# First block's startup: weights and modulation weights loaded each by its own free buffers, x transposed unscaled, contraction cut 3+5+8

## The chip, the cores and the metric

The kernel runs on one core of a Trainium2 chip. The metric is the device time of one execution in microseconds. Names of engines are those of the profile: PE (matrix), DVE (vector), ACT (scalar), POOL, and SP, which here only issues DMA.

## What is computed

The reference runs two transformer blocks, one after the other, on a sequence of 256 tokens of width 2048, in fp32. The change touches the beginning of the first block alone:

```python
mod = jax.nn.silu(c) @ w_ada[l] + b_ada[l]
shift1, scale1, gate1, shift2, scale2, gate2 = jnp.split(mod, N_MOD, axis=-1)

h = rms_norm(x, norm1_w[l]) * (1.0 + scale1[:, None]) + shift1[:, None]
proj = h @ w_in[l]
u_pool, q, k, v, g_a, g_b = jnp.split(proj, split_at, axis=-1)
```

`w_ada` has 2048 x 12288 elements and `w_in` 2048 x 8192. Behind that come a pooling branch, an attention branch, gates, an output projection and a feed-forward part; the second block has the same frame with other branches.

## The kernel before

All weights stream through one fixed sequence of blocks of 1 MiB, each a 128x4x512 fp32 tile `raw`. A matrix product is made of three products of rounded halves: ACT casts half a block (128x1024) to `hi` (fp32r, L201), DVE subtracts it from `raw` to get `lo` (L209), and PE runs hi, lo and hi again for each 128 of the contraction, each of 4 units of a block and each half of the tokens: 24 matmuls of 512 columns a block (L303 to L305). Half a block is called a sub. hi and lo have four buffers each, `raw` four.

Nothing is scheduled by the framework here: each engine executes in the order in which the code is written. `run` walks the subs; ahead of sub s it prepares hi and lo up to sub s+3 (`prep_to`, with `LOOK` = 3), then it issues the matmuls of sub s and, where a product ends there, its eviction.

The modulation is not a matrix product on PE. c is passed through silu and spread over all 128 partitions as `cb` (four matmuls with one active row, L497, copied from PSUM on DVE, L548). One column of 128 entries of `mod` is then one DVE operation, `ada_product` (L177): a 128x2048 tile of `w_ada` (1 MiB, `ada`, two buffers) times `cb`, summed along the row. In what follows that is a product.

The contraction of 2048 is cut in 16 slices k. Slice k of h, h tile k, needs products k and 16 + k; `h_tile` (L561) makes two columns `sAB` from them (DVE, L563, L565), and `modulate` (L381) makes act's high part on ACT (L384), hm on DVE (L385) and act's low part on DVE (L386).

So as not to need all 32 products at once, the first 48 blocks of `w_in` run in three chunks of the contraction (`CHUNKS` = 0, 4, 10, 16). In each chunk twelve column groups of 512 (ga 0 to 3, q, k, u and v, two each) are run over the chunk's k; in the first two chunks the four ga go k by k, in the last all go group by group. ga 0 and ga 1 keep their PSUM (`held`, tag ms); the others have two pairs of PSUM buffers in turn (tag acc) and put the partial sum in SBUF at each chunk's end: chunk 0 copies it on ACT (L607), the later ones add it on DVE (L609). Blocks 0 to 11 are chunk 0, 12 to 29 chunk 1, 30 to 47 chunk 2.

One queue holds the order of the weight blocks, the products and the calls; `when` says ahead of which block a product stands: two ahead of each of blocks 0 to 3, then from block 5 one each 1.1 blocks, from 19.5 one each 1.05. `pump` issues loads on SP strictly in that queue's order, and stops at the first one whose buffer isn't free. `prep_hi` executes the products and calls that stand ahead of a block before it casts the block's first half; so product, h tile, hi and lo stand in this order on DVE and ACT.

Of the kernel before, what the change touches and what calls it, by code (L numbers as in the profile page):

```python
# [18 lines left out]
P = 128  # L19
# [12 lines left out]
ADAB = 2  # L32

# [12 lines left out]
class Seg:  # L46
# [5 lines left out]
    def __init__(self, lhs, ks, end=None, tag="acc", end_tt=None, tail=2):  # L52
        self.lhs, self.ks, self.end, self.tag, self.end_tt = lhs, list(ks), end, tag, end_tt
        self.tail = tail if end_tt else 0
        self.acc = None
        self.left = [len(self.ks)] * 2

# [6 lines left out]
class Net:  # L64
    def __init__(self, ctx, tc, A):
# [21 lines left out]
        self.q_dma = 0  # L87
# [69 lines left out]
    def pump(self):  # L157

        while self.q_dma < len(self.queue):
            kind, what, src = self.queue[self.q_dma]  # L160
            if kind == "w":
                if what - self.prepped // 2 >= RAWB:
                    return
                t = self.rawp.tile([P, 4, 512], F32, tag="raw", name="raw")
                self.nc.sync.dma_start(out=t, in_=src)
                self.raw[what] = t
            elif kind == "a":
                if len(self.ada_dma) - self.ada_done >= ADAB:
                    return
                t = self.adap.tile([P, D], F32, tag="ada", name="ada")  # L170
                self.nc.sync.dma_start(out=t, in_=src)
                self.ada_dma.append(t)
            self.q_dma += 1
# [120 lines left out]
    def unit(self, seg, k, hi, lo, tts=(0, 1)):  # L294
        if seg.acc is None:
            seg.acc = [self.psp.tile([P, 512], F32, tag=seg.tag, name="acc") for _ in range(2)]
        for tt in tts:
            first = seg.left[tt] == len(seg.ks)
# [4 lines left out]
            self.nc.tensor.matmul(a, xh, hi, start=first, stop=False)  # L303
            self.nc.tensor.matmul(a, xh, lo, start=False, stop=False)  # L304
            self.nc.tensor.matmul(a, xl, hi, start=False, stop=last)  # L305
            if last and seg.end_tt:
                while self.pre_end:
                    self.pre_end.pop()()
                seg.end_tt(a, tt)
        if seg.end and not any(seg.left):  # L310
            seg.end(seg.acc)

# [171 lines left out]
    def setup(self):  # L484
        nc, fix, A = self.nc, self.fix, self.A

        row = self.mixp.tile([1, 2 * D], F32, tag="B", name="crow")
# [19 lines left out]
        self.mask = self.t2([P, P], name="mask")  # L507
        nc.sync.dma_start(out=self.mask, in_=A["mask"])
# [7 lines left out]
        self.mod2 = fix.tile([P, 96], F32, tag="mod2", name="mod2")  # L516

# [10 lines left out]
    def block1(self):  # L528
# [12 lines left out]
        junk = mp.tile([P, D], F32, tag="u", name="junk")  # L541
        for tt in range(2):
            nc.scalar.activation(junk, x[:, tt, :], AF.Square, accum_out=tot[:, tt:tt + 1])
            r = self.rstd(tot[:, tt:tt + 1], 1, D)
            nc.vector.tensor_scalar(out=x[:, tt, :], in0=x[:, tt, :], scalar1=r, scalar2=None, op0=ALU.mult)
            if tt == 0:
                for i, ps in enumerate(self.cbps):
                    nc.vector.tensor_copy(self.cb[:, i * 512:(i + 1) * 512], ps)  # L548
        nc.vector.scalar_tensor_tensor(out=wb, in0=self.pk("b_ada", 16, 16), scalar=1.0, in1=self.pk("norm1_w"),
                                       op0=ALU.add, op1=ALU.mult)  # L550
        xT = mp.tile([P, KD, S], F32, tag="B", name="xT")

        for tt in range(2):
            for c in range(4):
# [4 lines left out]
        self.at(6, self.setup2)  # L559

        def h_tile(k):  # L561
            sAB = self.fix.tile([P, 2], F32, tag="sAB", name="sAB", bufs=2)
            nc.vector.tensor_scalar(out=sAB[:, 0:1], in0=mod[:, 16 + k:17 + k], scalar1=self.pk("norm1_w", k, 1),  # L563
                                    scalar2=wb[:, k:k + 1], op0=ALU.mult, op1=ALU.add)
            nc.vector.tensor_tensor(out=sAB[:, 1:2], in0=mod[:, k:k + 1], in1=self.pk("b_ada", k, 1), op=ALU.add)  # L565
            self.modulate(xT[:, k, :], get(k // 4)[:, k % 4, :, :], sAB[:, 0:1], sAB[:, 1:2])
# [58 lines left out]

        held = {("ga", g): Seg(h_lhs, range(16), lambda acc, g=g: gate_a(g, acc), "ms") for g in range(2)}
        w = A["win1"]
        chunk = {}
# [3 lines left out]
        for c, (b0, every) in enumerate(((5, 1.1), (19.5, 1.05)), 1):  # L632
            for i in range(2 * (ch[c + 1] - ch[c])):
                when.setdefault(int(b0 + every * i), []).append((ch[c] + i // 2, i % 2))
        for nb, bl in enumerate(startup_blocks()):
# [7 lines left out]
            for key, k in bl:  # L643
                c = max(i for i in range(len(ch)) if ch[i] <= k)
                if key not in held and (key, c) not in chunk:
                    chunk[key, c] = Seg(h_lhs, range(ch[c], ch[c + 1]), part_end(key, c))
# [794 lines left out]
CHUNKS = (0, 4, 10, 16)  # L1441


def startup_blocks():
# [4 lines left out]
    for c in range(len(ch) - 1):  # L1449
# [4 lines left out]
        else:  # L1454
            rest = [keys[i] for i in (2, 3, 4, 0, 5, 1, 6, 8, 7, 9, 10, 11)]
# [99 lines left out]
```

## Time and profile before

| | us |
|---|---|
| median of 3 runs | 2512.89 |
| lowest and highest | 2510.8, 2512.9 |
| profiled execution | 2512.52 |
| its span, first to last instruction | 2510.7 |
| PE busy in the span | 2478.9 |
| PE idle in the first 300 us | 18.4 |

The page gives shares of the whole span; the windows view cuts the span in stretches and shows each engine's busy time in each, and there the idle time of PE is found at the start. The groups by line say how often an operation ran and how long the engine was idle before it; the timeline says when.

### The profile page before, as it was taken

What the parts mean: (1) busy time and instruction counts of PE and PEld (TensorE: products, weight loads), DVE (VectorE), ACT (ScalarE), POOL (GpSimd) and SP (SyncE); (2) the same over time, 40 slices, a digit from 0 to 9 for tenths busy, and PEclk for the clock granted to TensorE, in tenths of its full rate; (3) what the DMA queues carried; (4) which work ended last, traced back from release to release, by engine and by line L of the source; (5) the groups of instructions that cost most, each with busy time, mean ns of one, the idle gap of its engine ahead of it and who ended that gap; (6) DMA issues with size and microseconds to landing.
All of it is one profiled execution on the core that took longest, in us unless ns stands there. A gap on an engine that the chain in (4) does not pass through costs nothing.

```text
span 2510.7 us, 29213 instructions
## 1 busy us (share of the span) xinstructions
PE 2478.9 (99%) x11332; PEld 2047.1 (82%) x11332; DVE 1807.3 (72%) x2122; ACT 1259.9 (50%) x1727; POOL 4.0 (0%) x8
## 2 busy tenths in 40 slices
PE   7999999999999999999999999999999999999999
PEld 5778888887888888888887888888788888888887
DVE  7898888888875777787778878766676655456554
ACT  4536645445545444534446556665554453453443
POOL 0000000000000000000000000000000000000000
PEclk9999999999999999999999999999999999999999
DMA  9988678977887778787776655666567655555553
GB/s 358 369 322 318 243 297 323 394 306 286 303 317 284 303 315 316 287 333 306 294 276 222 249 214 211 221 232 223 212 252 278 259 200 194 208 185 191 193 190 130
DMA packets 93580, 666.24 MB, mean 265 GB/s; under 512 B 10817, under 2 KB 11521, under 8 KB 12929
## 3 DMA queue, kind: packets, MB, share of 16 engines
q1 hardware_dynamic: 93442, 664.38, 69.7%
q8 instruction: 89, 1.46, 0.2%
q14 instruction: 49, 0.40, 0.0%
HBM read 660.11 MB, written 4.23 MB: 265 GB/s over the span
## 4 chain that ended last, share of the span: by engine, by line
PE 88%; DVE 6%; ACT 3%; DMA 1%; issue 1%; SPq 0%; ACTq 0%; DVEq 0%
PE acc L303 28%; PE acc L305 28%; PE acc L304 28%; DVE lo L209 2%; DVE ada L177 2%; PE ms L348 1%; DMA raw<-in_win 1%; ACT hi L201 1%; PE ms L1178 1%; PE ms L855 1%; PE ms L1292 0%; ACT hm L1396 0%; PE ms L1410 0%; DVE res L395 0%; PE ms L762 0%
## 5 line engine op out<-in xcount | busy, mean ns | idle before, releaser
L209 DVE TENSOR_TENSOR lo<-raw,hi 128x1024 fp32r<-128x1024 f32 x848 | 1027.6, 1223 | 594.7 <-ACT hi L201 591.6
L201 ACT CAST hi<-raw 128x1024 fp32r<-128x1024 f32 x848 | 884.7, 1051 | 868.1 <-PE acc L305 825.0
L303 PE MATMUL acc<-hi,act 128*128 128x512 f32 x2208 | 875.5, 396 | 7.6 <-ACT hi L201 6.1
L304 PE MATMUL acc<-lo,act 128*128 128x512 f32 x2208 | 864.3, 391 | 9.8 <-DVE lo L209 9.8
L305 PE MATMUL acc<-hi,act 128*128 128x512 f32 x2208 | 863.1, 391 | 0.0
L304 PEld LDWEIGHTS acc<-lo,act 128*128 128x128 f32 x2208 | 416.3, 189 | 99.7 <-DVE lo L209 17.2
L303 PEld LDWEIGHTS acc<-hi,act 128*128 128x128 f32 x2208 | 416.2, 188 | 94.9 <-ACT hi L201 8.4
L305 PEld LDWEIGHTS acc<-hi,act 128*128 128x128 f32 x2208 | 415.9, 188 | 88.1 <-DVE act L1401 0.7
L177 DVE CUSTOM_DVE_ANT_0 ada<-ada,cb 128x2048 f32<-128x2048 f32 x192 | 438.3, 2284 | 0.5 <-DMA ada<-in_ada 0.5
L303 PE MATMUL acc<-hi,f 128*128 128x512 f32 x1024 | 399.1, 390 | 0.0
L305 PE MATMUL acc<-hi,f 128*128 128x512 f32 x1024 | 398.4, 389 | 0.0
L304 PE MATMUL acc<-lo,f 128*128 128x512 f32 x1024 | 398.4, 389 | 0.0
L305 PEld LDWEIGHTS acc<-hi,f 128*128 128x128 f32 x1024 | 192.2, 188 | 40.1
L304 PEld LDWEIGHTS acc<-lo,f 128*128 128x128 f32 x1024 | 192.2, 188 | 39.9
L303 PEld LDWEIGHTS acc<-hi,f 128*128 128x128 f32 x1024 | 192.2, 188 | 39.1
L384 ACT ACTIVATE act<-xT,sAB 128x256 fp32r<-128x256 f32 x16 | 9.6, 601 | 86.2 <-DVE sAB L565 86.2
L419 ACT ACTIVATE relu<-acc 128x512 f32<-128x512 f32 x64 | 37.7, 590 | 29.0 <-PE acc L305 29.0
L350 DVE TENSOR_TENSOR f<-ms,f 128x512 fp32r<-128x512 f32 x64 | 41.0, 683 | 3.1 <-ACT f L349 3.1
L395 DVE TENSOR_TENSOR res<-acc,gate 128x512 f32<-128x512 f32 x32 | 22.0, 689 | 28.2 <-PE acc L305 28.2
L398 ACT ACTIVATE res<-x 128x512 f32<-128x512 f32 x24 | 15.2, 633 | 52.6 <-DVE x L396 52.6
L420 ACT ACTIVATE relu<-relu 128x512 f32<-128x512 f32 x64 | 40.5, 633 | 2.0
L349 ACT CAST f<-ms 128x512 fp32r<-128x512 f32 x64 | 34.4, 589 | 13.8 <-PE ms L348 13.8
(245 smaller groups left out, 1266.8 us busy)
## 6 DMA issues: line engine op xcount, KB each, us to landing
raw<-in_ff SPq DMA_DIRECT2D x240, 1024.0 KB, 5.6
ada<-in_ada SPq DMA_DIRECT2D x192, 1024.0 KB, 5.8
raw<-in_win SPq DMA_DIRECT2D x120, 1024.0 KB, 6.5
raw<-in_ff1p SPq DMA_DIRECT2D x16, 1024.0 KB, 4.8
raw<-in_wa SPq DMA_DIRECT2D x8, 1024.0 KB, 6.9
raw<-in_wb SPq DMA_DIRECT2D x8, 1024.0 KB, 9.1
raw<-in_wop SPq DMA_DIRECT2D x8, 1024.0 KB, 6.9
raw<-in_wo SPq DMA_DIRECT2D x8, 1024.0 KB, 9.7
```

The costliest lines, as they stand in the source:

```text
L177: self.nc.vector.tensor_tensor_reduce(out=t, in0=t, in1=cb(), scale=1.0, scalar=0.0, op0=ALU.mult, op1=ALU.add, accum_out=mod[:, j:j + 1])
L201: self.nc.scalar.copy(hi, src)
L209: self.nc.vector.tensor_tensor(out=lo, in0=src, in1=hi.bitcast(F32), op=ALU.subtract)
L303: self.nc.tensor.matmul(a, xh, hi, start=first, stop=False)
L304: self.nc.tensor.matmul(a, xh, lo, start=False, stop=False)
L305: self.nc.tensor.matmul(a, xl, hi, start=False, stop=last)
L348: nc.tensor.transpose(ps[:, i, :], src[:, i * P:(i + 1) * P], self.ident)
L349: nc.scalar.copy(dst[:, :, 0, :], ps)
L350: nc.vector.tensor_tensor(out=dst[:, :, 1, :], in0=ps, in1=dst[:, :, 0, :].bitcast(F32), op=ALU.subtract)
L419: nc.scalar.activation(r, acc[tt], AF.Relu)
L420: nc.scalar.activation(r, r, AF.Square)
L855: mm = lambda *a, **kw: nc.tensor.matmul(*a, skip_group_check=True, **kw)
```

## The change

- `pump` keeps a list of weight loads and one of modulation loads. Each is issued when a buffer of its own kind is free, the one that stands first in the queue first. The first four modulation tiles lie in the four buffers of act (`ADAX`), which are empty then, so six modulation loads and four weight loads can be out at the start.
- The mask's load moves from the start to sub 4, and `setup2`, which reads it, from sub 6 to sub 10.
- Two matmuls of a blank 128x512 tile stand ahead of the four that spread c.
- x is no longer scaled by the reciprocal norm before it is transposed. The scale of each token is spread over the partitions by two transposes as `rows`, and h tile multiplies by it: hm is one operation of two tensors and a column on DVE, then act's high part on ACT, then its low part on DVE. The two columns of `sAB` are made on ACT.
- `CHUNKS` is 0, 3, 8, 16: blocks 0 to 8, 9 to 23, 24 to 47. In the last chunk ga 2 and ga 3 go k by k first. `when` starts at block 3 with one product a block, and at block 13 with one each 0.92.
- Chunk 1 no longer adds on DVE: when a pair of PSUM buffers is evicted, ACT copies the next group's partial sum from SBUF into it (`back`, `heir`), the matmuls add onto it, and ACT copies the sum out again. Chunk 2 adds on DVE as before.

```diff
+ADAX = 4
...
+    def open(self, net):
+
+        self.acc = [net.psp.tile([P, 512], F32, tag=self.tag, name="acc") for _ in range(2)]
+        if self.init:
+            self.init(self.acc)
...
+        if self.loads is None:
+            self.loads = {kind: [i for i, e in enumerate(self.queue) if e[0] == kind][::-1] for kind in "wa"}
+        ws, ads = self.loads["w"], self.loads["a"]
+        while True:
+            n = len(self.ada_dma)
+            w = ws and self.queue[ws[-1]][1] - self.prepped // 2 < RAWB
+            a = ads and (n < ADAX + ADAB or n - self.ada_done < ADAB)
+            if w and (not a or ws[-1] < ads[-1]):
+                _, b, src = self.queue[ws.pop()]
+                t = self.raw[b] = self.rawp.tile([P, 4, 512], F32, tag="raw", name="raw")
+            elif a:
+                src = self.queue[ads.pop()][2]
+
+                if n < ADAX:
+                    t = self.actp.tile([P, D], F32, tag="act", name="ada")
+                else:
+                    t = self.adap.tile([P, D], F32, tag="ada", name="ada")
                 self.ada_dma.append(t)
-            self.q_dma += 1
+            else:
+                return
+            self.nc.sync.dma_start(out=t, in_=src)
...
         if seg.end and not any(seg.left):
             seg.end(seg.acc)
+            if seg.heir:
+                seg.heir.open(self)
...
+        ps = self.ms()
+        for i in range(2):
+            nc.tensor.matmul(ps, blank[:, 0:P], blank, start=i == 0, stop=i == 1)
...
-            nc.vector.tensor_scalar(out=x[:, tt, :], in0=x[:, tt, :], scalar1=r, scalar2=None, op0=ALU.mult)
...
+            nc.scalar.activation(sa, mod[:, 16 + k:17 + k], AF.Identity, bias=wb[:, k:k + 1],
+                                 scale=self.pk("norm1_w", k, 1))
+            nc.scalar.activation(sb, mod[:, k:k + 1], AF.Identity, bias=self.pk("b_ada", k, 1))
+            h = self.t2([P, S], name="hm")
+            nc.vector.scalar_tensor_tensor(out=h, in0=src, scalar=sa, in1=rows, op0=ALU.mult, op1=ALU.mult)
+            nc.scalar.activation(dst[:, 0, :], h, AF.Identity, bias=sb)
+            nc.vector.scalar_tensor_tensor(out=dst[:, 1, :], in0=h, scalar=sb, in1=dst[:, 0, :].bitcast(F32),
+                                           op0=ALU.add, op1=ALU.subtract)
...
-                    if c == 0:
+                    if c < len(ch) - 2:
                         nc.scalar.copy(d[:, tt, :], acc[tt])
...
+        def back(key):
+            def init(acc):
+                d = part(key)
+                for tt in range(2):
+                    nc.scalar.copy(acc[tt], d[:, tt, :])
+            return init
...
-        for c, (b0, every) in enumerate(((5, 1.1), (19.5, 1.05)), 1):
+        for c, (b0, every) in enumerate(((3, 1.0), (13, 0.92)), 1):
...
+                    if 0 < c < len(ch) - 2:
+                        seg.init = back(key)
+                        order[-3].heir = seg
...
-CHUNKS = (0, 4, 10, 16)
+CHUNKS = (0, 3, 8, 16)
...
-            rest = [keys[i] for i in (2, 3, 4, 0, 5, 1, 6, 8, 7, 9, 10, 11)]
+            out += [(g, k) for k in ks for g in keys[2:4]]
+            rest = [keys[i] for i in (0, 4, 1, 5, 6, 8, 7, 9, 10, 11)]
```

Where instructions stand now. First SP, the queue of loads at the program's start; `ada` is a modulation load, `raw` a weight load. Before:

```order
L508 DMA mask<-in_mask 128x128
L171 DMA ada<-in_ada 128x2048 x2
L165 DMA raw<-in_win 128x2048
L171 DMA ada<-in_ada 128x2048 x2
L165 DMA raw<-in_win 128x2048
L171 DMA ada<-in_ada 128x2048 x2
L165 DMA raw<-in_win 128x2048
```

After:

```order
L531 DMA pkt<-in_pk 128x293
L189 DMA ada<-in_ada 128x2048 x2
L189 DMA raw<-in_win 128x2048
L189 DMA ada<-in_ada 128x2048 x2
L189 DMA raw<-in_win 128x2048
L189 DMA ada<-in_ada 128x2048 x2
L189 DMA raw<-in_win 128x2048 x4
L189 DMA ada<-in_ada 128x2048 x2
L189 DMA raw<-in_win 128x2048
```

Six modulation loads and six weight loads now stand ahead of the seventh modulation load (the first of the last `ada` row); the mask's load has moved behind.

Second DVE, from the product ahead of block 13's lo on; the `ISA` rows with `ada` are the products (each with the read-out of its column), `hm` and `act` belong to an h tile, `lo` x2 is a block. Before, blocks 13 to 15:

```order
L177 ISA ada,mod_113<-ada,cb 128x2048
L177 ISA mod_113 128x1
L209 TENSOR_TENSOR lo<-raw,hi 128x1024 x2
L177 ISA ada,mod_113<-ada,cb 128x2048
L177 ISA mod_113 128x1
L563 TENSOR_SCALAR sAB<-mod_113,pkt,wb 128x1
L565 TENSOR_TENSOR sAB<-mod_113,pkt 128x1
L385 TENSOR_SCALAR hm<-xT,sAB 128x256
L386 TENSOR_TENSOR act<-hm,act 128x256
L209 TENSOR_TENSOR lo<-raw,hi 128x1024 x4
```

After, blocks 13 to 15:

```order
L193 ISA ada,mod_115<-ada,cb 128x2048
L193 ISA mod_115 128x1
L193 ISA ada,mod_115<-ada,cb 128x2048
L193 ISA mod_115 128x1
L601 SCALAR_TENSOR_TENSOR hm<-xT,sAB,rrow 128x256
L603 SCALAR_TENSOR_TENSOR act<-hm,sAB,act 128x256
L225 TENSOR_TENSOR lo<-raw,hi 128x1024 x2
L193 ISA ada,mod_115<-ada,cb 128x2048
L193 ISA mod_115 128x1
L225 TENSOR_TENSOR lo<-raw,hi 128x1024 x2
L193 ISA ada,mod_115<-ada,cb 128x2048
L193 ISA mod_115 128x1
```

In before blocks 14 and 15 have one product between them; in after block 13 has two, and blocks 14 and 15 one each (block 15's h tile and lo follow these rows).

Third ACT, in after, from block 13 to block 16: `sAB` and `act` are an h tile's, `hi` a sub each, `gap<-acc` the eviction of ga 2 and ga 3 at the end of chunk 1, `acc<-qk` the partial sums put back for q and k:

```order
L217 CAST hi<-raw 128x1024 x4
L597 ACTIVATE sAB<-mod_115,wb,pkt 128x1
L599 ACTIVATE sAB<-mod_115,pkt 128x1
L602 ACTIVATE act<-hm,sAB 128x256
L217 CAST hi<-raw 128x1024
L645 COPY gap<-acc 128x512 x2
L668 COPY acc<-qk 128x512 x2
L645 COPY gap<-acc 128x512 x2
L668 COPY acc<-qk 128x512 x2
L217 CAST hi<-raw 128x1024 x3
```

In before, where the adds of chunk 1 are on DVE, ACT has nothing but h tiles and hi between chunk 0's last eviction and block 31:

```order
L384 ACTIVATE act<-xT,sAB 128x256
L201 CAST hi<-raw 128x1024 x6
L384 ACTIVATE act<-xT,sAB 128x256
L201 CAST hi<-raw 128x1024 x6
L384 ACTIVATE act<-xT,sAB 128x256
L201 CAST hi<-raw 128x1024 x4
```

The evictions of block 13 and the copies back now stand on ACT behind the h tile and the first hi of block 15, and ahead of its second hi.

## Rows read from the trace of the kernel before

**Rows 1.** The page, part 1: busy us, share of the span, instructions.

```profile
PE 2478.9 (99%) x11332; PEld 2047.1 (82%) x11332; DVE 1807.3 (72%) x2122; ACT 1259.9 (50%) x1727; POOL 4.0 (0%) x8
```

**Rows 2.** Busy time by windows: busy us, granted clock, DMA share, GB/s.

```profile
0.00:10.00 10.00, 5.63 (x7) 2.49 (x8) 1.74 (x8) 8.52 (x8) 0.20 (x4) 1.00 0.80 301
...
20.00:30.00 10.00, 8.38 (x24) 6.34 (x25) 8.49 (x12) 3.72 (x6) 0.00 (x0) 0.66 0.92 360
...
200.00:250.00 50.00, 50.00 (x225) 41.27 (x224) 38.33 (x46) 31.31 (x64) 0.00 (x0) 1.00 0.79 298
```

**Rows 3.** Waits of PE in the first 205 us: total, times, longest.

```profile
PE acc L304 <- DVE lo L209: 6.5, 9, 0.8
PE acc L303 <- ACT hi L201: 6.1, 3, 3.1
...
PE acc L303 <- DVE gap L609: 1.1, 1, 1.1
```

**Rows 4.** Groups on DVE, 41.0 to 167.7 us: count, busy, mean ns, idle before.

```profile
L209 DVE TENSOR_TENSOR lo<-raw,hi 128x1024 fp32r<-128x1024 f32 x43 | 51.6, 1222 | 10.8 <-ACT hi L201 10.8
L177 DVE CUSTOM_DVE_ANT_0 ada<-ada,cb 128x2048 f32<-128x2048 f32 x20 | 45.7, 2284 | 0.5 <-DMA ada<-in_ada 0.5
L386 DVE TENSOR_TENSOR act<-hm,act 128x256 fp32r<-128x256 f32 x10 | 4.3, 426 | 2.2 <-ACT act L384 2.2
...
L609 DVE TENSOR_TENSOR qk<-acc,qk 128x512 f32<-128x512 f32 x6 | 3.8, 680 | 0.0
...
L609 DVE TENSOR_TENSOR gap<-acc,gap 128x512 f32<-128x512 f32 x4 | 2.5, 682 | 0.0
```

**Rows 5.** DVE in order of time: start, us, operation, idle before.

```profile
25.61 2.29 DVE L177 CUSTOM_DVE_ANT_0 ada<-ada,cb 128x2048 f32<-128x2048 f32 x1
27.83 0.08 DVE L177 DVE_READ_ACCUMULATOR2_ANT mod<- 128x1 f32 x1
...
29.89 2.36 DVE L209 TENSOR_TENSOR lo<-raw,hi 128x1024 fp32r<-128x1024 f32 x2 [0.51 <-ACT hi L201]
32.17 2.29 DVE L177 CUSTOM_DVE_ANT_0 ada<-ada,cb 128x2048 f32<-128x2048 f32 x1
...
40.94 2.28 DVE L177 CUSTOM_DVE_ANT_0 ada<-ada,cb 128x2048 f32<-128x2048 f32 x1
```

**Rows 6.** ACT in order of time, same columns.

```profile
10.40 0.29 ACT L334 ACTIVATE rstd<-sstot,eps 128x1 f32<-128x1 f32 x1
...
28.32 0.60 ACT L384 ACTIVATE act<-xT,sAB 128x256 fp32r<-128x256 f32 x1 [6.28 <-DVE sAB L565]
28.83 1.98 ACT L201 CAST hi<-raw 128x1024 fp32r<-128x1024 f32 x2
...
54.60 2.04 ACT L607 COPY gap<-acc 128x512 f32<-128x512 f32 x4
56.51 1.08 ACT L201 CAST hi<-raw 128x1024 fp32r<-128x1024 f32 x1
```

**Rows 7.** DVE again: a lo behind ACT's copies.

```profile
57.62 1.23 DVE L209 TENSOR_TENSOR lo<-raw,hi 128x1024 fp32r<-128x1024 f32 x1 [1.10 <-ACT hi L201]
```

**Rows 8.** DVE around block 24, in order of time.

```profile
167.73 2.36 DVE L209 TENSOR_TENSOR lo<-raw,hi 128x1024 fp32r<-128x1024 f32 x2 [0.52 <-ACT hi L201]
```

**Rows 9.** PE in order of time: first matmuls of blocks 5, 6, 24, 30.

```profile
60.81 0.39 PE L303 MATMUL acc<-hi,act 128*128 128x512 f32 x1
...
66.25 0.39 PE L303 MATMUL acc<-hi,act 128*128 128x512 f32 x1
...
167.81 0.45 PE L303 MATMUL acc<-hi,act 128*128 128x512 f32 x1
...
204.29 0.39 PE L303 MATMUL acc<-hi,act 128*128 128x512 f32 x1
```

**Rows 10.** Busy time by windows, 2 us each: DMA at its fullest.

```profile
50.00:52.00 2.00, 2.00 (x11) 1.63 (x10) 2.00 (x9) 0.84 (x1) 0.00 (x0) 1.00 1.01 426
```

More of the change, by code (lines that the diff above doesn't have):

```diff
@@ L86, in __init__ @@
         self.pre_end = []
-        self.q_dma = 0
+        self.loads = None
         self.q_use = 0
@@ L295, in unit @@
         if seg.acc is None:
-            seg.acc = [self.psp.tile([P, 512], F32, tag=seg.tag, name="acc") for _ in range(2)]
+            seg.open(self)
         for tt in tts:
-            first = seg.left[tt] == len(seg.ks)
+            first = seg.left[tt] == len(seg.ks) and not seg.init
             seg.left[tt] -= 1
@@ L302, in unit @@
             a = seg.acc[tt]
-            self.nc.tensor.matmul(a, xh, hi, start=first, stop=False)
-            self.nc.tensor.matmul(a, xh, lo, start=False, stop=False)
-            self.nc.tensor.matmul(a, xl, hi, start=False, stop=last)
+            mm = lambda *o, **kw: self.nc.tensor.matmul(a, *o, skip_group_check=bool(seg.init), **kw)
+            mm(xh, hi, start=first, stop=False)
+            mm(xh, lo, start=False, stop=False)
+            mm(xl, hi, start=False, stop=last)
             if last and seg.end_tt:
@@ L516, in setup, with load_mask @@
         self.mod2 = fix.tile([P, 96], F32, tag="mod2", name="mod2")
+    def load_mask(self):
+        self.mask = self.t2([P, P], name="mask")
+        self.nc.sync.dma_start(out=self.mask, in_=self.A["mask"])
     def setup2(self):
@@ L558, in block1 @@
                 nc.scalar.copy(xT[:, 4 * c:4 * c + 4, tt * P:(tt + 1) * P], ps)
-        self.at(6, self.setup2)
+        ps = self.ms([P, 2, P])
+        for tt in range(2):
+            nc.tensor.transpose(ps[:, tt, :], r[tt].to_broadcast([P, P]), self.ident)
+        nc.scalar.copy(rows, ps.rearrange("p a b -> p (a b)"))
+        self.at(4, self.load_mask)
+        self.at(10, self.setup2)
         def h_tile(k):
             sAB = self.fix.tile([P, 2], F32, tag="sAB", name="sAB", bufs=2)
[L563 to L566, printed above, removed]
+            sa, sb = sAB[:, 0:1], sAB[:, 1:2]
+            src, dst = xT[:, k, :], get(k // 4)[:, k % 4, :, :]
+            nc.scalar.activation(sa, mod[:, 16 + k:17 + k], AF.Identity, bias=wb[:, k:k + 1],
[6 more added lines that the diff above has]
+                                           op0=ALU.add, op1=ALU.subtract)
         def need(k):
@@ L624, in part_end @@
             return end
+        def back(key):
+            def init(acc):
+                d = part(key)
+                for tt in range(2):
+                    nc.scalar.copy(acc[tt], d[:, tt, :])
+            return init
         held = {("ga", g): Seg(h_lhs, range(16), lambda acc, g=g: gate_a(g, acc), "ms") for g in range(2)}
         w = A["win1"]
[L628 removed]
+        chunk, order = {}, []
         ch = CHUNKS
         when = {}
[L632 removed]
+        for c, (b0, every) in enumerate(((3, 1.0), (13, 0.92)), 1):
             for i in range(2 * (ch[c + 1] - ch[c])):
@@ L645, in block1 @@
                 if key not in held and (key, c) not in chunk:
-                    chunk[key, c] = Seg(h_lhs, range(ch[c], ch[c + 1]), part_end(key, c))
+                    seg = chunk[key, c] = Seg(h_lhs, range(ch[c], ch[c + 1]), part_end(key, c))
+                    order.append(seg)
+                    if 0 < c < len(ch) - 2:
+                        seg.init = back(key)
+                        order[-3].heir = seg
                 units.append((held[key] if key in held else chunk[key, c], k))
```

35 lines of the change are left out of this document (12 added, 23 removed).

## The prediction

> **What bounds the kernel now.** First the page: PE is busy 99% of the span [rows 1], so what can be won or lost is idle PE time. The windows put much of that at the start: PE is busy 5.63 and 8.38 us of the slices shown there, and all 50 us from 200 us on [rows 2]. PE's waits up to 205 us are for `lo`, for `hi` and once for the eviction of a chunk [rows 3]. So the start runs at the pace of whoever makes hi, lo and h, and the view to read next is DVE in the stretch from 41 to 167.7 us, in which it makes lo number 6 to 47 [rows 4]: 20 modulation products, 42 lo (the row's 43 has one that was running at 41.0), ten h tiles, ten adds of a partial sum, and 10.8 us idle behind ACT's hi. I take the first lo of block 24, lo 48, as the milestone: 167.73 us [rows 8], and PE starts block 24 at 167.81 and then waits for it [rows 9].
>
> PE unhindered takes 66.25 - 60.81 = 5.44 us for a block of 24 matmuls [rows 9]. From block 5 to block 30 that would be 136.0 us; it took 204.29 - 60.81 = 143.5. So before loses 7.5 us there, 3.8 of it from block 24 to 30 (36.5 against 32.6).
>
> **Prices on DVE** [rows 5]. One product: from lo at 29.89 with two lo to the product at 32.17 is 2.28, so 1.14 a lo; product 25.61 to its read-out's end is 2.29, and the next product can start after 2.21 (27.83 less 25.61, within 0.01). Product with h tile: 25.61 to the lo at 29.89 is 4.28, so h adds 2.07, 0.51 of it waiting for hi. An add is 6.3 / 10 = 0.63 [rows 4].
>
> **The start, up to 41 us.** The change takes the scaling of x off DVE, copies cb first, adds two blank matmuls ahead of cb's and two transposes behind x's, and moves the mask's load. All that can bring the first product forward from 14.6 us, by 3 us at best. I cost it at nothing, since a load comes after it: ten loads are now issued at once, and the seventh modulation load (k = 3) can't start before the fifth product frees its buffer; in SP's order it is the 13th of these loads. Ahead of its end stand 2 MiB of x, 0.27 MB of tables and 13 MiB of loads: 16.0 MB. By 10 us 3.0 MB are moved [rows 2]; DMA at its fullest moves 426 GB/s [rows 10], so the other 13.0 MB take 30.5 us and the load ends near 40.5, about 41 with its landing. By DVE's order six products, six lo and three h lie ahead of it, ended by about 39.4 to 41.6, whichever way the clock stands. Before, the seventh product starts at 40.94 with the same six products, six lo and three h done [rows 5]. So both kernels stand at the same point at 41 us, and from there one sum compares them. The blank matmuls cost at most 0.4 us of cb's matmuls; a gain from a warmer clock there is covered by that load too.
>
> The Trainium skill, page "DMA: Bandwidth & Descriptors", section Specifications, gives one core's share of HBM as about 358 GB/s. By it the 13.0 MB would take 36.3 us and the whole chain would come 5.8 later; the trace's 426 GB/s disagrees, and the sum goes by the trace.
>
> **From 41 us to lo 48, against before.** After puts two products ahead of block 13 and two ahead of block 24, one ahead of each other block: 30 products and 15 h ahead of lo 48, where before has 26 and 13. Since chunk 2 now starts at block 24 and asks for eight new k in four blocks, the products must come earlier; before spreads them to block 31.
> - Four more products: 4 x 2.21 = +8.8.
> - Two more h: 2 x 2.07 = +4.1.
> - Each of the 12 h in this stretch is dearer. The two columns of sAB are made on ACT, then hm on DVE, act on ACT, and only then hi. The chain from a product's start to its lo: 2.29, ACT's one-column activation about 0.29 (the one with a bias) [rows 6], a 128x256 two-tensor operation 0.43 [rows 4], the start of act to hi 0.51 (28.83 - 28.32) [rows 6], hi 1.06 (28.83 to 29.89) [rows 5, 6], hand-overs 0.1: 4.68 against 4.28. So 12 x 0.4 = +4.8. The new forms are not in the trace: were the one-column step free, it would be 0.1 each (not below, since hm now runs ahead of act and not beside it), and with half as much again for both new steps 0.75 each, so +1.2 to +9.0; I take the chain, whose rows are the nearest in shape.
> - Ten adds go to ACT: -6.3.
> - DVE's waits behind ACT that are no h wait. Before: 10.8 less 10 x 0.515 is 5.6, with 0.5 for a load 6.2 [rows 4]. After, ACT has more copies between the two hi of a block that has an h. With n copies there at 0.48 each (54.60 to 56.51 for four) and 0.95 for hi, less the 1.14 of the lo that runs meanwhile, the second lo waits 0.48 n - 0.19 [rows 6]; a four-copy place before shows 1.10 [rows 7]. ACT's order has such places at blocks 4 (n = 4), 8 (2), 10 (4, two of them the new copies back into PSUM), 15 (8) and 19 (4): 1.7 + 0.8 + 1.7 + 3.6 + 1.7 = 9.5. The difference is +3.3. A copy from SBUF into PSUM is not in the trace; I take the 0.48 of the eviction. At nothing it would take 3.8 off, at 0.6 add 1.
>
> Sum +14.8 (8.8 + 4.1 + 4.8 - 6.3 + 3.3): lo 48 at 182.5.
>
> The same places hold PE up directly: the key after the first two of chunk 1 adds onto copies that ACT makes behind the h of block 15, so PE idles ahead of block 14, some 7 us after block 13 by this chain, and ahead of block 3 likewise. Those stops are no second charge; PE only waits for the same chain. A stop costs clock too: behind the 3.1 us wait at the start [rows 3] the granted clock is 0.66 in the slice [rows 2], part of it at the lower of the two levels, 1.2 GHz. PE has DVE's lead to make that up, so I add nothing, and up to 2 us on the range's upper side.
>
> **After block 24.** Before still loses 3.8 us to block 30. After has two products left and then none until block 37; I count 1.1 for the second key of block 24, which waits for v's copies behind three hi, and 0.2 for block 26: 1.3. Later blocks fill PE in both; unscaled x, the mask and the loads' order change no matmul there.
>
> Sum: 14.8 - 3.8 + 1.3 = +12.3. Loads of weights no longer stand behind modulation loads: that takes away part of ACT's waits for raw, which are in the 6.2 that I took off already.
>
> **Rivals.**
> - DVE is the limit but ACT's copies are hidden: the 9.5 and the 1.1 fall away. +14.8 - 9.5 - 3.8 + 0.2 = +1.7: 2514. For it: ACT is half idle [rows 1]. Against: it executes in order, and rows 7 shows the wait.
> - Faster. The shorter first chunk gives PE full work from block 3 on and DVE keeps up. Block 3 starts when the first chunk's copy ends: product 41.0 + 2.2 + two lo 2.3, product and h to hi 3.6, hi 0.95, copy 0.6: 50.7, against 60.81 - 2 x 5.44 = 49.9 before. With nothing lost afterwards that is +0.8 - 7.5 = -6.7: 2506. It decides at the point where two blocks of DVE (2 x 2.21 + 4 x 1.14 + 2.47 = 11.5) fit into two of PE (10.9); they don't, and two blocks hold a second product on top.
> - The first loads come at 360 GB/s, as in the slice from 20 us [rows 2]: 36.1 us for the 13.0 MB, the seventh load 5.6 later, the whole chain with it: 2530.5, and up to 2 more where later products wait for their loads too. Against: that slice held a pause between loads (DMA share 0.92).
> - The separate issue does nothing and the costs cancel: within 2 us of before.
>
> **How the numbers follow.** The sum is against the profiled execution, 2512.5 (span 2510.7 and 1.8 around it): 2524.8; the runs' median is 0.4 above it, so 2525. Chances: the forecast (2518 to 2530) 0.62, hidden copies 0.14, faster 0.10, late loads 0.09, no effect 0.05. The range 2513 to 2531 leaves out the faster case and about half of the late one. Measurement can tell 0.2% from no change, 5 us. Faster 0.10; same 0.14 + 0.05 = 0.19; slower 0.71.
>
> **What would show it.** In the changed kernel's profile: the seventh product at 41 us; lo 48 near 182; a product's start to its lo 4.7 with an h; the second lo of block 15 some 3.6 behind hi; PE idle ahead of block 14. DVE idle between blocks 27 and 37. It is wrong if lo 48 comes before 172, if the seventh product starts well before 39, or if PE's total idle time falls below that of before.

## The result: 0.8% slower, and where the profile after puts it

| | before | after |
|---|---|---|
| median of 4 runs, us | 2511.99 | 2530.93 |
| lowest and highest | 2510.8, 2512.9 | 2529.64, 2534.2 |
| profiled execution | 2512.52 | 2529.64 |
| its span | 2510.7 | 2527.9 |
| PE busy in the first 300 us | 281.60 | 273.82 |

The ratio is 1.0078, 95% interval 1.006 to 1.0095. The forecast was 2525.0. The direction and the chain through DVE hold, but the size was too small by 6 us: the median lies at the very top of the range (2531), and the ratio on the earlier median of 2512.89 gives 2532.5, beyond it. One step was wrong in kind as well, the clock behind PE's stop at block 24.

PE's waits up to 225 us, to be read against [rows 3]:

```profile
PE acc L319 <- ACT hi L217: 9.1, 4, 3.2
PE acc L319 <- ACT acc L668: 4.3, 1, 4.3
PE acc L319 <- DVE lo L225: 4.0, 7, 0.8
PE acc L319 <- ACT v L645: 3.9, 2, 3.4
PE acc L319 <- ACT gap L645: 2.6, 1, 2.6
```

New are waits for ACT's copies, out of PSUM (L645) and back into it (L668). The groups on DVE from 41.0 to 186.4 us, against [rows 4]:

```profile
L193 DVE CUSTOM_DVE_ANT_0 ada<-ada,cb 128x2048 f32<-128x2048 f32 x24 | 54.8, 2286 | 0.9 <-DMA ada<-in_ada 0.9
L225 DVE TENSOR_TENSOR lo<-raw,hi 128x1024 fp32r<-128x1024 f32 x44 | 52.5, 1222 | 15.3 <-ACT hi L217 15.3
L603 DVE SCALAR_TENSOR_TENSOR act<-hm,sAB,act 128x256 fp32r<-128x256 f32 x12 | 5.8, 485 | 7.7 <-ACT act L602 7.7
L601 DVE SCALAR_TENSOR_TENSOR hm<-xT,sAB,rrow 128x256 f32<-128x256 f32 x12 | 5.8, 485 | 5.5 <-ACT sAB L597 5.5
```

Four more products and two more h stand there, no add, and 15.3 us behind hi where before had 10.8. DVE after it is done with the products, against the last of [rows 2] (DVE 38.33 there): it has run ahead of its work, and PE is full.

```profile
200.00:250.00 50.00, 50.00 (x226) 41.41 (x225) 29.28 (x33) 31.49 (x50) 0.00 (x0) 1.00 0.59 209
```

The milestones, DVE in order of time: the seventh product, a product with an h, and lo 48 (before at 167.73, [rows 8]).

```profile
42.38 2.29 DVE L193 CUSTOM_DVE_ANT_0 ada<-ada,cb 128x2048 f32<-128x2048 f32 x1
...
46.87 2.29 DVE L193 CUSTOM_DVE_ANT_0 ada<-ada,cb 128x2048 f32<-128x2048 f32 x1
49.08 0.08 DVE L193 DVE_READ_ACCUMULATOR2_ANT mod<- 128x1 f32 x1
49.62 0.48 DVE L601 SCALAR_TENSOR_TENSOR hm<-xT,sAB,rrow 128x256 f32<-128x256 f32 x1 [0.46 <-ACT sAB L597]
50.74 0.48 DVE L603 SCALAR_TENSOR_TENSOR act<-hm,sAB,act 128x256 fp32r<-128x256 f32 x1 [0.64 <-ACT act L602]
51.67 1.22 DVE L225 TENSOR_TENSOR lo<-raw,hi 128x1024 fp32r<-128x1024 f32 x1 [0.45 <-ACT hi L217]
...
186.45 1.22 DVE L225 TENSOR_TENSOR lo<-raw,hi 128x1024 fp32r<-128x1024 f32 x1 [0.45 <-ACT hi L217]
```

Where a stop of PE comes from shows at blocks 24 and 14. At block 24, ACT in order of time, then the first matmul on PE:

```profile
183.98 0.39 ACT L597 ACTIVATE sAB<-mod,wb,pkt 128x1 f32<-128x1 f32 x1 [6.38 <-DVE mod L193]
184.27 0.28 ACT L599 ACTIVATE sAB<-mod,pkt 128x1 f32<-128x1 f32 x1
184.97 0.51 ACT L602 ACTIVATE act<-hm,sAB 128x256 fp32r<-128x256 f32 x1 [0.42 <-DVE hm L601]
185.39 1.03 ACT L217 CAST hi<-raw 128x1024 fp32r<-128x1024 f32 x1
186.32 1.06 ACT L645 COPY v<-acc 128x512 f32<-128x512 f32 x2
```

```profile
186.95 0.63 PE L319 MATMUL acc<-hi,act 128*128 128x512 f32 x1 [3.44 <-ACT v L645]
```

ACT stands idle for 6.38 us because the h tile waits for DVE's product; v's sums, done in PSUM, stand behind it, and PE behind them. But block 24's own hi stands behind the same h and ends only at 186.42, so of the 3.44 us the copies of v cost PE the last 0.5. At block 14 it is the copies alone: its hi and lo are done by 119.6, and PE waits for the copies back for q and k, which stand behind the h of block 15 (the h's act at 122.81, `acc<-qk` at 125.12):

```profile
125.77 0.80 PE L319 MATMUL acc<-hi,act 128*128 128x512 f32 x1 [4.28 <-ACT acc L668]
```

To compare kernels I use one number, the lag of a block: the start of its first matmul less 5.435 us for each block before it (24 matmuls unhindered, [rows 9]). Where the lag stands still, PE is full. From block 33 on PE also has groups of eight transposes of q and k between blocks, 0.9 to 1.1 us each, which raise the lag too; by block 40 after has run three of them, before two, e7, e9 and e12 one, so the last column is to be read with that. The lag is counted from PE's rows; us:

```
block                                4     12     15     24     30     40
before                            33.5   33.7   36.0   37.4   41.2   43.3
after                             36.0   38.1   51.4   56.5   58.7   61.5
e5 new cut and order alone        35.8   35.9   47.8   56.7   63.5   66.3
e4 loads alone                    34.2   34.2   35.5   36.9   40.8   42.8
e2 after, old h tile              37.5   38.3   50.2   52.7   54.4   57.1
e1 after, old cut and order       37.5   46.8   46.8   48.7   51.5   53.6
e3 after, adds on DVE             37.7   38.7   52.5   63.9   71.2   73.9
e6 adds on ACT alone              34.5   42.0   42.0   42.3   44.7   46.7
e15 the same, copy back later     33.0   33.2   35.4   35.7   38.2   40.2
e8 after, products spread         39.3   41.4   45.1   45.5   46.8   51.7
e7 before, products spread        33.0   33.2   34.9   36.3   36.3   40.1
e9 the same, ga 2 and 3 first     32.5   32.8   34.7   36.1   36.2   37.6
e12 the same in every chunk       32.5   32.6   34.1   34.1   34.1   35.7
```

Over before's, after's lag is 4.4 at block 12, 15.4 at block 15, 19.1 at block 24 and 17.5 at block 30: most of it comes between blocks 12 and 15.

### The profile page after: what moved, and what is told of

It is laid out like the page before. It is cut to its first block, busy times and chain, and to the rows that moved or that the text cites. A ratio compares the mean times of both kernels' runs of the same rounds, so it can differ in the third digit from the quotient of the medians.

```text
span 2527.9 us, 29213 instructions
## 1 busy us (share of the span) xinstructions
PE 2486.8 (98%) x11338; PEld 2050.6 (81%) x11338; DVE 1790.1 (71%) x2069; ACT 1285.0 (51%) x1798; POOL 4.0 (0%) x8
## 4 chain that ended last, share of the span: by engine, by line
PE 89%; DVE 6%; ACT 3%; issue 1%; DMA 1%; SPq 0%; ACTq 0%; DVEq 0%
PE acc L319 83%; DVE lo L225 2%; DVE ada L193 2%; PE ms L367 1%; ACT hi L217 1%; PE ms L1227 1%; PE ms L904 1%; DMA ada<-in_ada 1%; PE ms L1341 0%; ACT hm L1445 0%; PE ms L1459 0%; PE ms L855 0%; PE ms L522 0%; PE ms L811 0%; DVE hm L601 0%
## 5 line engine op out<-in xcount | busy, mean ns | idle before, releaser
L319 PE MATMUL acc<-hi,act 128*128 128x512 f32 x4416 | 1406.4, 394 | 20.6 <-ACT hi L217 9.1
L319 PE MATMUL acc<-hi,f 128*128 128x512 f32 x2048 | 634.1, 389 | 0.0
L319 PE MATMUL acc<-hi,pT 128*128 128x512 f32 x128 | 42.8, 399 | 0.0
L439 ACT ACTIVATE relu<-relu 128x512 f32<-128x512 f32 x64 | 40.5, 633 | 2.0
L597 ACT ACTIVATE sAB<-mod,wb,pkt 128x1 f32<-128x1 f32 x16 | 6.2, 390 | 69.3 <-DVE mod L193 69.3
L319 PE MATMUL acc<-hi,oT 128*128 128x512 f32 x128 | 40.6, 391 | 0.0
L403 ACT ACTIVATE act<-ms,shiftc,sA 128x256 fp32r<-128x256 f32 x36 | 20.3, 563 | 39.0 <-DVE hm L404 32.8
L367 PEld LDWEIGHTS ms<-cst,relu 128*128 128x128 f32 x256 | 29.8, 140 | 4.2
```

Of the source, the lines that this page charges most:

```text
L319: mm = lambda *o, **kw: self.nc.tensor.matmul(a, *o, skip_group_check=bool(seg.init), **kw)
L367: nc.tensor.transpose(ps[:, i, :], src[:, i * P:(i + 1) * P], self.ident)
L439: nc.scalar.activation(r, r, AF.Square)
```

## The experiments

Each was run beside before on one chip; before's median was 2511.0 to 2511.7 throughout.

**Which part costs.** e1 puts the old cut, order and `when` into after; e5 puts the new ones into before; e4 puts the separate issue of loads (and `ADAX`) alone into before; e2 gives after the scaled x and before's h tile.

```diff
 # e5_schedule_alone, on before (e1: the reverse, on after)
-CHUNKS = (0, 4, 10, 16)
+CHUNKS = (0, 3, 8, 16)
...
-            rest = [keys[i] for i in (2, 3, 4, 0, 5, 1, 6, 8, 7, 9, 10, 11)]
+            out += [(g, k) for k in ks for g in keys[2:4]]
+            rest = [keys[i] for i in (0, 4, 1, 5, 6, 8, 7, 9, 10, 11)]
...
-((5, 1.1), (19.5, 1.05))
+((3, 1.0), (13, 0.92))
```

> Before with only the new schedule: chunks 3+5+8, its spacing of products and its order in the last chunk; adds of chunk 1 stay on DVE, h tile and loads as before. Theory A: ahead of lo 48 four more products (+8.8), two more h (+4.1), six more adds (+3.8) and a four-copy place at block 4 (+1): lo 48 near 185 us, time 2524 to 2532 us. Theories B and C: within 5 us of before.

> The changed kernel with the schedule of before: chunks 4+6+6, products spaced 1.1 and 1.05 blocks from blocks 5 and 19.5, the last chunk's groups in the old order; all else stays (loads apart, unscaled x, adds of chunk 1 on ACT). Theory A (the time is lost because the new schedule asks DVE for 30 products ahead of block 24 and all 32 ahead of block 26): ahead of lo 48 stand 26 products and 13 h again, so lo 48 falls from 186.5 us to 166 to 171 us and the time to 2510 to 2516 us. Theory B (the dearer h tile, 4.80 us from product to lo against 4.28, is the cause): the h tile is still there, so most of the 19 us stays, 2522 us or more. Theory C (the copies of chunk 1 on ACT): they are still there too, 2522 or more.

> The changed kernel with x scaled before the transposes and the h tile of before; schedule, loads and ACT copies stay. Theory A: from the seventh product on 12 h tiles ahead of lo 48 get 0.52 us cheaper and the seventh product starts about 1.4 us earlier; lo 48 near 179 us, time 2521 to 2525 us. Theory B: back to about 2512 us. Theory C: 2526 us or more.

> Before with only the separate issue of weight and modulation loads. All theories that blame another part: DVE's few waits behind late weights (some 2 us of the 6.2) go, 2508 to 2512 us. If the separate issue itself costs time (loads of one kind holding up the other), 2515 us or more.

Measured: e5 2536.02 (ratio 1.0095, 1.008 to 1.011), e1 2522.78 (1.0043, 1.0026 to 1.0059), e2 2526.48 (1.0061, 1.0046 to 1.0076), e4 2512.75 (1.0004, 0.9995 to 1.0013). So the new cut and order alone cost 24 us, more than the whole change. e5 is 4 us above its own range although its lo 48 (185.16) is where it was expected; behind that, PE waits 7.1 us for v's adds on DVE at block 24. The h tile costs 4.5 net (2530.93 less 2526.48). That is less than the 6.2 by which twelve h got cheaper (0.52 each): e2's lo 48 is at 182.61 and not near 179, since DVE there waits 2.5 us more for hi and for loads, and e2's time misses its range. e4 is just above its range; the loads do nothing to the time that can be told. The rest of the change without the h tile gives some 10 of it back (e2 against e5). e1 missed: taking the new cut out again leaves 11 of 19. Why is the next question.

**The adds on ACT.** e3 puts chunk 1's adds in after back on DVE; e6 moves them to ACT in before, nothing else.

```diff
 # e3_adds_on_dve, on after (e6: the reverse with open, init and heir, on before)
-                    if c < len(ch) - 2:
+                    if c == 0:
                         nc.scalar.copy(d[:, tt, :], acc[tt])
...
-                    if 0 < c < len(ch) - 2:
+                    if False:
                         seg.init = back(key)
```

> The changed kernel with chunk 1's partial sums added on DVE again, as before; all else as changed. Theory C (ACT's copies out and back into PSUM behind the h tile are what costs): PE no longer waits for them, 2512 to 2518. Theory A (the new cut asks for more products ahead of block 24, so DVE is the limit), by the prediction's own terms: ten adds +6.3, the DVE waits behind those copies at blocks 10 and 15 about -4.5, so 2530 to 2534. By the two runs in hand (the new cut with adds on DVE +24, with adds on ACT and the old h tile +15): 9 more than the changed kernel, 2536 to 2542.

> The kernel before, with only chunk 1's adds moved from DVE to ACT's copies out and back. Theory DVE alone: ten adds of 0.63 us leave the engine that sets the pace, 2506 to 2508. Theory copies: chunk 0's last evictions and the copies back stand on ACT behind an h tile, PE waits for them ahead of block 11 as it did with the old cut (6.1 us for the copies of v), 2517 to 2521: of the 11 us that the changed kernel with the old cut loses, what the h tile's 4 leave.

Measured: e3 2542.87 (1.0124, 1.0109 to 1.0139), e6 2515.44 (1.0016, 1.0006 to 1.0026). Theory C falls: without ACT's copies after is 12 slower. DVE's groups of e3 up to block 24 give the size, 8 + 4 + 4 + 2 = 18 adds:

```profile
L647 DVE TENSOR_TENSOR qk<-acc,qk 128x512 f32<-128x512 f32 x8 | 5.1, 682 | 0.0
L647 DVE TENSOR_TENSOR u<-acc,u 128x512 f32<-128x512 f32 x4 | 2.6, 681 | 0.0
L647 DVE TENSOR_TENSOR gap<-acc,gap 128x512 f32<-128x512 f32 x4 | 2.5, 681 | 0.0
...
L647 DVE TENSOR_TENSOR v<-acc,v 128x512 f32<-128x512 f32 x2 | 1.3, 682 | 0.0
```

18 at 0.63 is 11.3, near the 12, but not all of it comes that way. Lo 48 of e3 is only 6.0 us later than after's (192.42 against 186.45): 16 of the adds stand ahead of it, and some 3.4 us of DVE's waits for hi and for loads are gone in return. The other 6 come behind it, where the seventh matmul of block 24 waits for the adds of v:

```profile
PE acc L319 <- DVE v L647: 3.9, 1, 3.9
```

So the move to ACT is the good part of the change, needed because the new cut ends chunk 1 ahead of block 24. My own terms in that expectation (+6.3 for ten adds) had taken before's count. With the old cut (e6) the time lies between the two theories. There the same move loses 7.5 of lag at one place, a stop ahead of block 11 and the slow block behind it, and gains 4.8 from there to block 30 (2.7 where before has 7.5). ACT of e6 in order of time, and PE's stop:

```profile
97.89 0.60 ACT L395 ACTIVATE act<-xT,sAB 128x256 fp32r<-128x256 f32 x1 [3.88 <-DVE sAB L576]
98.40 1.03 ACT L209 CAST hi<-raw 128x1024 fp32r<-128x1024 f32 x1
99.34 1.06 ACT L618 COPY v<-acc 128x512 f32<-128x512 f32 x2
100.29 1.11 ACT L641 COPY acc<-gap 128x512 f32<-128x512 f32 x2
```

```profile
99.96 0.80 PE L311 MATMUL acc<-hi,act 128*128 128x512 f32 x1 [5.53 <-ACT v L618]
```

Block 11 is v's second group. In before it has the PSUM pair of the group two ahead, free long since; why it now waits for the first v, one group ahead, had two answers: that ACT's copies stand behind an h, or that the copy back takes the free pair. Two runs on that:

```diff
 # e13_adds_on_act_heirs, on e6 (e14_after_heirs: the same on after)
-                    if 0 < c < len(ch) - 2:
-                        seg.init = back(key)
-                        order[-3].heir = seg
+                    if c < len(ch) - 2:
+                        if c:
+                            seg.init = back(key)
+                        if len(order) > 2:
+                            order[-3].heir = seg
 # e15_adds_on_act_late, on e6
+                        if c == 1 and key == ("ga", 2):
+                            order[-2].late = seg
+                        else:
+                            order[-3].heir = seg
...
+        if seg.late:
+            seg.late.open(self)
+            seg.late = None
         if seg.end and not any(seg.left):
```

> The kernel before with chunk 1's adds moved to ACT's copies, as in the run of that part alone (+4.3), but with the PSUM pairs handed on in one order: each group of chunk 0 takes its pair when the group two ahead is evicted, so that the copy back for ga 2 no longer takes the pair that the last group of chunk 0 would have had. Theory pairs: the last group of chunk 0 no longer waits for v's copies behind the h tile; the 5.5 us and the clock behind it (8.3 of lag by block 12) fall to 1 or less, and the 4.8 that DVE saves from block 12 to 30 stay: lag of block 30 36 to 39, 2506 to 2510. Theory copies (what costs is that ACT's copies stand behind an h tile, whichever pair): within 2 of 2515.4.

> The changed kernel with the PSUM pairs handed on in one order in the same way. At the end of its chunk 0 no h tile stands ahead of the copies, PE waits there 0.6 and 0.4 us and the lag grows by 2.1 from block 7 to 10, so theory pairs gives at most 2: 2528.5 to 2530.5; the stops at blocks 14 and 24 come from copies behind an h tile and stay. Theory copies: 2530 to 2532. If both stops go, 2522 or less.

> The kernel before with chunk 1's adds on ACT's copies, where the first copy back (for ga 2) is written only after the first unit of chunk 0's last group has run. A PSUM pair is given out at its first write, so that group now gets the pair that was evicted a block earlier, and the copy back the one whose copies stand behind the h tile. Theory pairs: PE's 5.5 us ahead of block 11 and the clock behind it go, lag of block 12 near 35, of block 30 36 to 39, 2506 to 2510. Theory copies (ACT's copies behind an h tile cost, whoever waits for them): a stop of the same kind moves to block 12 or 13, 2513 to 2516.

Measured: e13 2515.34 (1.0014, 1.0006 to 1.0023) and e14 2532.96 (1.0087, 1.0072 to 1.0102): no gain, and in e13 the stop stayed (5.4 us for v, lag 40.9 at block 12). The edit had not done what it said: PE still waits for the copies of v's first group, so the second still took that group's pair. Neither run tests a theory. The reading is that a buffer is given out at its first write, not where it is asked for. e15 moves the first write: 2510.16 (0.9995, 0.9986 to 1.0004), 5.3 less than e6, no wait for v (its waits from 45 to 300 us):

```profile
PE acc L312 <- DVE lo L218: 3.4, 5, 0.8
PE acc L312 <- ACT hi L210: 0.4, 1, 0.4
PE acc L312 <- ACT gap L622: 0.4, 1, 0.4
```

The copies of v stand behind the same h tile; what changed is the pair, and the first copy back comes one hi later. So theory pairs holds for e6. e1 has the same stop (6.1 us for v, lag 38.1 at block 10 and 46.8 at 12); that it has the same cause is argued, as e1 was not run with the later copy back. In after the pairs of chunk 0 can cost 2 us at most (its lag from block 7 to 10). At block 14 q takes the pair that ga 2 has just left, at block 24 ga 2 that of v, both evicted behind an h. That the copies' place counts there is read from ACT's rows above; no run moves those copies, and none gives q another pair.

**The start.** e11 takes the two blank matmuls out of after.

> The changed kernel without the two blank matmuls ahead of cb's. Prediction's step (the start is bound by the seventh modulation load, what comes before it is covered): first product within 1 us of the changed kernel's 14.1, seventh within 1 us of its 42.4, time within 2 us of it, 2528 to 2533. Rival (the blank matmuls set the clock of the start, or hold it back): the start shifts by 1.5 to 3 us and the time with it.

Measured 2531.66 (1.0079, 1.0063 to 1.0094): the same as after. The seventh product, in e3, where DVE was ready early, and in e11:

```profile
42.30 2.29 DVE L193 CUSTOM_DVE_ANT_0 ada<-ada,cb 128x2048 f32<-128x2048 f32 x1 [2.28 <-DMA ada<-in_ada]
```

```profile
42.31 2.29 DVE L193 CUSTOM_DVE_ANT_0 ada<-ada,cb 128x2048 f32<-128x2048 f32 x1 [1.04 <-DMA ada<-in_ada]
```

e1 has it at 42.53 behind 2.55 us. Whatever the start gains, that load takes back. e4 shows that the new issue alone puts it there: it has the seventh product at 42.62, behind 1.60 us for its load, where before has it at 40.94.

**Products asked for later.** e8 lets after's last chunk run all four ga k by k, so that one new k is needed per block, and spreads the products. e7 does the same in before; e9 puts ga 2 and ga 3 ahead in each k but the first, so that their sums are evicted under ga 0 and ga 1; e12 does so in all chunks; e10 is e9 with the adds of q, k, u and v on ACT.

```diff
 # e8_after_spread, on after
-((3, 1.0), (13, 0.92))
+((3, 1.0), (13, 1.18))
...
-            out += [(g, k) for k in ks for g in keys[2:4]]
-            rest = [keys[i] for i in (0, 4, 1, 5, 6, 8, 7, 9, 10, 11)]
+            out += [(g, k) for k in ks for g in keys[:4]]
+            rest = [keys[i] for i in (4, 5, 6, 8, 7, 9, 10, 11)]
 # e12_order_all, on before (e7: keys[:4] in place of the order by k; e9: the last chunk alone)
-((5, 1.1), (19.5, 1.05))
+((5, 1.1), (19.5, 1.38))
...
-            out += [(g, k) for k in ks for g in keys[:4]]
+            out += [(keys[i], k) for k in ks for i in ((2, 3, 0, 1) if k > ks[0] else (0, 1, 2, 3))]
...
-            rest = [keys[i] for i in (2, 3, 4, 0, 5, 1, 6, 8, 7, 9, 10, 11)]
+            out += [(keys[i], k) for k in ks for i in ((2, 3, 0, 1) if k > ks[0] else (0, 1, 2, 3))]
+            rest = [keys[i] for i in (4, 5, 6, 8, 7, 9, 10, 11)]
```

> The changed kernel with ga 0 to ga 3 k by k in the last chunk (one new k a block in blocks 24 to 31) and its products one each 1.18 blocks from 13 in place of 0.92. Theory A (DVE is held by products asked for too early): 2 to 3 products and one h less ahead of block 24 and none of the pairs at blocks 13 and 24, 2519 to 2525. Theory C (the copies behind the h tile of block 15 are what costs, they stay): 2528 to 2531.

> The kernel before, with the last chunk running ga 0 to ga 3 k by k (one new k a block in blocks 30 to 35) and, since they are then needed later, its products one each 1.38 blocks from 19.5 in place of 1.05. Theory A (products ahead of their need are what DVE can't hold): about 2.5 products and one h less ahead of block 30, the start lag of block 30 falls from 41 to 37, 2507 to 2509. Rival (the evictions that now come together at block 36 take it back): the lag gained is lost by block 48, 2511 to 2515. If DVE is not the limit: 2512 within 1.

> As the kernel before with the last chunk's ga 0 to ga 3 k by k and products one each 1.38 blocks, but ga 2 and ga 3 ahead of ga 0 and ga 1 in each k but the first, so that their sums are added while ga 0 and ga 1 still run. Theory A (DVE and what waits for it): the start lag of block 30 stays near 36.4 and PE's 2.0 us ahead of block 36 go, 2507 to 2510. Rival (the time is spent elsewhere after block 30, whatever the lag): 2511.5 to 2513.

> The same, with chunk 1's partial sums of q, k, u and v (not those of ga) copied out and back by ACT as in the changed kernel. Theory A with the copies harmful only where they stand behind an h tile and ahead of a chunk's first keys: the 5.5 us ahead of block 11 don't come, DVE has 5 us less to do between blocks 18 and 29, block 30's lag 35 to 36, 2506 to 2509. Theory C (copies on ACT cost wherever they are): 2513 or more.

> As the kernel before with the last chunk's ga 0 to ga 3 k by k (ga 2 and ga 3 first) and products one each 1.38 blocks, and now ga 2 and ga 3 ahead of ga 0 and ga 1 in the first two chunks as well (each k but a chunk's first). Theory A (PE's last stops are for sums that stand on DVE behind an h tile): the 1.1 us ahead of block 18 go, with their clock some 1.2 us of the lag of 36 at block 24, 2506.5 to 2509. Rival (the order of the units changes nothing that the end depends on): as without this edit, 2509 to 2511.

Measured: e8 2520.86 (1.0039, 1.0026 to 1.0052), 10 less than after. From the seventh product to lo 48 (173.53) it has 21 products and 10 h, where after has 24 and 12. e7 2512.12 (1.0004, 0.9995 to 1.0014) missed its range: its lag at block 30 falls by 4.9 as expected, but at block 44, where both kernels have run three groups of transposes, it is 43.5 where before has 44.2. PE is idle for 2.0 of that ahead of block 36, where two sums are added at once: the rival. e9 2509.60 (0.9992, 0.9983 to 1.0001) and e10 2510.59 (0.9995, 0.9986 to 1.0003) can't be told from before; e9 has a lag of 41.1 at block 44. e10's lag at block 4 was already 2.8 above e9's, ahead of any moved add, so what its adds bring is open. e12 2507.20 (0.9985, 0.9976 to 0.9994) is faster than both kernels (39.1 at block 44), by 0.15% against before. Its PE waits from 45 to 300 us are all that is left:

```profile
PE acc L304 <- DVE lo L209: 1.9, 4, 0.6
PE ms L762 <- DVE qk L746: 0.3, 1, 0.3
PE acc L303 <- DVE v L609: 0.3, 1, 0.3
```

## Where the prediction was right, and which step failed

- **DVE as the limit, products asked for too early: right.** e5 (+24) and e8 (-10 from the other side) show it. The rival with hidden copies (2514) and the faster one (2506) fall with rows: lo 48 at 186.45, and PE's idle time in the first 300 us is 26.2, not 18.4. The second lo of block 15 (3.73 behind hi) and PE's stop ahead of block 14 came as named.
- **The seventh product at 41.0: 42.38, +1.4.** The start was put at nothing, since both kernels would stand at the same point at 41 us; they did not. The load is the bound, as said, but lands at 42.3; bytes over rate had given 40.5, and 0.5 for the landing was too little. From 0 to 42.35 us DMA moved 398 GB/s, 16.9 MB, where I had counted 16.0 up to this load's end; by estimate the other 0.9 MB belong to the load issued behind it, and at 426 GB/s they take 2 us. The DVE chain, with h at its new price, came as late. DMA ran at its full rate meanwhile, so the late-loads rival falls; that its time (2530.5) came close is luck:

```profile
20.00:30.00 10.00, 7.64 (x24) 5.57 (x24) 7.94 (x9) 3.66 (x7) 0.00 (x0) 0.83 1.02 429
```

- The Trainium skill's figure for one core's share (page "DMA: Bandwidth & Descriptors", section Specifications, about 358 GB/s) disagrees with this row too; the sum was right to go by the trace.
- **h dearer by 0.4: 0.52, +1.4 over twelve.** 46.87 to 51.67 is 4.80, not 4.68 (before 4.28): the two-tensor operations with a column take 0.48 and not 0.43, and ACT's first column 0.39 and not 0.29.
- **Waits behind ACT's copies of 9.5: right; DVE's waits for hi in all 9.9, +0.4.** 15.3 less twelve times 0.45. The five places took 1.67, 0.68, 1.73, 3.73 and 1.72, together 9.5. The other 0.38 stands ahead of block 16's second lo (134.20), whose hi had waited 1.68 us for PE: that much of PE's stop at block 14 did come back to DVE. The eight copies at block 15, priced at 3.6:

```profile
129.25 1.23 DVE L225 TENSOR_TENSOR lo<-raw,hi 128x1024 fp32r<-128x1024 f32 x1 [3.73 <-ACT hi L217]
```

- **Products never wait for loads after 41 us: 0.9.** Not in the sum: 0.50 at 115.00, behind the pair of products at block 13, and 0.39 at 181.64, in the pair at block 24. The prediction gave no reason for putting these waits at nothing.
- **A slip in the other direction, -0.5.** From before's 10.8 us behind hi [rows 4] I took ten waits of an h, but only nine lie in that window; the tenth stands ahead of lo 48 itself. Before's other waits are 6.7, not 6.2, and the difference should have been +2.8. The terms so far are 1.4 + 1.4 + 0.4 + 0.9 - 0.5 = 3.6, and lo 48 came 3.95 late; the rest is not followed.
- **From block 24 to 30 a loss of 1.3: 2.6, and this step was wrong in kind.** 0.4 is that block 24 itself started 0.5 behind its lo (before 0.1), for v's copies. The other 2.2 is lag, 2.0 of it in block 24. The wait that I had charged, 1.1 for the second key behind v's copies, did not come: from 183 to 225 us PE waits for v once, the 3.4 ahead of block 24. What came is the clock, which I had put at nothing because DVE's lead would let PE make it up. PE behind that stop, and the window around it:

```profile
187.73 0.80 PE L319 MATMUL acc<-lo,act 128*128 128x512 f32 x1
188.32 1.05 PE L319 MATMUL acc<-hi,act 128*128 128x512 f32 x2
189.18 0.63 PE L319 MATMUL acc<-lo,act 128*128 128x512 f32 x1
```

```profile
187.00:191.00 4.00, 3.85 (x10) 2.63 (x11) 3.31 (x3) 4.00 (x6) 0.00 (x0) 0.57 0.55 219
```

The first eight matmuls of block 24 take 3.8 us (186.95 to 190.76), where eight at the full pace take 1.8, and the granted clock is 0.57, most of it at the lower level. Some 0.3 of the 2.0 is the second matmul's wait for lo 48, which ends at 187.67; the other 1.7 is by estimate the clock. Ahead of block 24 a slow PE only waits less for DVE's chain afterwards, but from here on PE is full and nothing gives the time back. That is read from these rows; no run takes this stop alone away. e8, which has no stop ahead of block 24, loses 1.3 up to block 30, 1.0 of it in a wait for v.
- **Adds -6.3: right as a difference from before**, for the reason that e3 shows: 18 adds would otherwise stand ahead of block 24, 16 of them ahead of lo 48.

With these the lag of block 30 is 12.3 + 3.95 + 1.3 = 17.55 above before's; measured are 17.5, and 17.2 in the span. The runs' median lies 1.3 above the profiled execution, where 0.4 was assumed, which adds 0.9 to the miss of the forecast. So what failed is the size of the sum at four terms: the start put at nothing (1.4), the h tile at 0.4 (0.52, 1.4 over twelve), waits for loads put at nothing (0.9), and the stretch behind block 24 at 1.3 (2.6). Behind the last stands a wrong mechanism, a wait for copies in place of the clock; in the others the mechanism held and the price was too low.

## What to carry to other kernels

An engine that executes in order couples what stands on it: an eviction written behind a step that waits for another engine makes PE wait for that engine, so count the wait in front of a copy and not only the copies. The slow clock behind a stop costs little while PE waits for another engine's chain anyway, and counts in full once PE is the limit. When a contraction is cut in chunks, count by which block each chunk's inputs are due and spread their making up to that point; the best version here (e12) does less early work, not faster work. Handing buffers on early can take the free one from the next user: see in the built program who has which.

## What was not expected of the hardware

The eight one-row matmuls that spread c took 7.19 us in after and 4.05 in e1, with the same instructions ahead of them. PE in order of time, first after, then e1:

```profile
1.45 3.78 PE L514 MATMUL ms<-crow 128*128 128x512 f32 x4 [1.45 <-DVE crow L508]
5.16 7.19 PE L522 MATMUL ms<-crow 1*128 1x512 f32 x8
```

```profile
1.45 3.78 PE L514 MATMUL ms<-crow 128*128 128x512 f32 x4 [1.45 <-DVE crow L508]
5.16 4.05 PE L522 MATMUL ms<-crow 1*128 1x512 f32 x8
```

That is a factor of 1.8, where the two clock levels (1.2 and 2.4 GHz) lie a factor of 2 apart, but the granted clock reads 1.00 in both stretches (5 to 9 us), so what differs is not shown. Of the six profiles with the blank matmuls ahead, four (e1, e2, e3, e14) took 3.9 to 4.1 us and two (after, e8) 7.19; the eleven without them all took 7.19. So the blank matmuls may shorten the start, but not each time, and e11 compares two kernels that both took 7.19; in e1 and e3, which took the short form, the seventh modulation load took the gain back. A stop later on costs clock, as the prediction feared. The window from 110 us, which begins with the 2.5 us stop ahead of block 13:

```profile
110.00:120.00 10.00, 7.38 (x19) 5.48 (x20) 8.33 (x9) 4.51 (x7) 0.00 (x0) 0.66 0.91 343
```

The granted clock is 0.66, so part of it lies at the lower level, and block 13's 24 matmuls take from 112.15 to 121.49, where 5.44 is the full pace (0.5 of it is a wait for lo).
